# The right half of slice 0's G: from the software queue with a cast to SP's queue and a rounding on VectorE

## The chip, the cores and the metric

The kernel runs on one core of a Trainium2 chip. The metric is the device time of one execution in microseconds. Before the change the median of three runs is 163.8 us (163.7 to 163.8). The profile is one execution, recorded by the hardware profiler.

## The reference

The gradient of a weight, summed over batch and rows:

```
input       : (16, 512, 1024) float32      X, seen as 8192 x 1024
grad_output : (16, 512, 768)  float32      G, seen as 8192 x 768
grad_weight = einsum('bmk,bmn->kn', input, grad_output)      1024 x 768, float32
```

So it is one matrix product, X transposed times G, contracted over 8192 rows. The kernel multiplies in bf16 and accumulates in float32.

## The kernel before, in words

**Slices and units.** The 8192 rows are cut into 64 slices of 128 rows; two neighbouring slices make a unit (32 units). A slice of X is 128 x 1024 (512 KB in float32), a slice of G 128 x 768 (384 KB). The output is split into quarters: A and B are the left half of X's columns with the left and the right half of G's, C and D the right half of X's with the left and the right half of G's. Each quarter has four blocks of 128 x 384, one per PSUM bank, and two quarters are open at a time.

**Two kinds of units.** `LOADS` (line 12) gives the first seven and the last two units the kind "s": each slice is multiplied as it is. The other 23 are of kind "P": VectorE forms sums and differences of the unit's quarters (lines 126 to 155), and seven products, named A, D, m, n, o, p and q, take the place of eight.

**The order.** `ORDER` (line 16) is a list of visits written out by hand. "C2:4!0,0,0,0" opens quarter C, brings it up to item 2 (slices 0 and 1), lets ScalarE empty 4 of its banks, and closes it. The first visits are A1 (slice 0), D1 (slice 0, left open), C2 (slices 0 and 1), B2 (slices 0 and 1), D3 (slices 1 and 2), A2, B4, A3, C4 and A4; D5 is the first to use slice 4 (unit 2) and B7 the first to use slice 6 (unit 3). A visit to one slice is four matmuls, to two slices eight. In C2 the first matmul uses slice 0, the second slice 1, and so on in turn. Work on TensorE, VectorE, ScalarE and GpSimd (POOL) goes in the order in which it is written (line 77). When a quarter is closed, each bank is emptied by a copy or an addition (lines 295 to 304).

**The loads.** From unit 2 on, POOL issues one transfer of G and one of X for each unit, float32 in memory and bf16 in SBUF (lines 105 and 106): this is queue q0, the software queue, in the profile. Slices 1 to 3 of G and slices 2 and 3 of X come the same way, slice by slice (lines 112 and 114). The start is different. X of slices 0 and 1 and the left half of slice 0's G come in float32 over hardware queues, into the staging tiles `xf` and `gf` (lines 79 to 83): the left half of G and then X of slice 1 from SP (queue q1), X of slice 0 from ScalarE (queue q10). They are rounded to bf16 by VectorE and ScalarE (`round_by`, line 205; for slice 0 in lines 210 to 216, for slice 1 in lines 362 to 365 just before C2). The right half of slice 0's G is the first transfer of POOL (line 110) and is rounded on the way in.

**The start of TensorE.** Twelve matmuls on constants (`WARMUP`, line 88) run while the first loads are under way. Then A1 needs the left half of slice 0's X and of its G, D1 the right halves of both, C2 the right half of X and the left half of G of slices 0 and 1, and B2 the other halves of the same two slices.

Of the kernel before, what the change touches and what calls it, by code (L numbers as in the profile page):

```python
# [9 lines left out]
P = 128  # L10
# [32 lines left out]
def kernel(  # L43
# [6 lines left out]
    nc = tc.nc  # L50
# [4 lines left out]
    _, _, N = grad_output.shape  # L55
    S = B * M // P
    KH = K // 2
    NH = N // 2
# [3 lines left out]
    G = grad_output.rearrange("b m n -> (b m) n")  # L62
# [17 lines left out]
    gf = pairs.tile([P, N], f32, name="gf", tag="gp")  # L80
    nc.sync.dma_start(out=gf[:, 0:NH], in_=G[0:P, 0:NH])
    nc.scalar.dma_start(out=xf[0], in_=X[0:P, :])
    nc.sync.dma_start(out=xf[1], in_=X[P : 2 * P, :])

    ones = nc.const_aps.tensor(1.0, (P, P), bf16)
# [13 lines left out]
    for u, kind in enumerate(LOADS):  # L99
        pool = pairs if u else head  # L100
        xp = pool.tile([P, 2, K], bf16, name="xp", tag="xp")
        gp = pool.tile([P, 2, N], bf16, name="gp", tag="gp")
        if u >= MERGED:
            rows = slice(2 * u * P, 2 * (u + 1) * P)
            nc.gpsimd.dma_start(out=gp, in_=G[rows, :].rearrange("(p m) n -> p m n", m=2))  # L105
            nc.gpsimd.dma_start(out=xp, in_=X[rows, :].rearrange("(p m) k -> p m k", m=2))  # L106
        for h in range(2):
            s = 2 * u + h
            if s == 0:
                nc.gpsimd.dma_start(out=gp[:, 0, NH:N], in_=G[0:P, NH:N])  # L110
            if s > 0 and u < MERGED:
                nc.gpsimd.dma_start(out=gp[:, h, :], in_=G[s * P : (s + 1) * P, :])
            if s > 1 and u < MERGED:
                nc.gpsimd.dma_start(out=xp[:, h, :], in_=X[s * P : (s + 1) * P, :])
            if kind == "s":
                items.append(("s", xp[:, h, :], gp[:, h, :]))
        if kind == "P":
            items.append(("P", xp, gp))
        xg.append((xp, gp))
# [79 lines left out]
    def fill(n):  # L199
        for _ in range(n):  # L200
            f, i = filler.pop()
            f(i)


    def round_by(engine, dst, src, c0, c1):
        copy = nc.vector.tensor_copy if engine == "DVE" else nc.scalar.copy
        copy(out=dst[:, c0:c1], in_=src[:, c0:c1])

    x0, x1, g0 = items[0][1], items[1][1], items[0][2]
# [144 lines left out]
    for n, step in enumerate(ORDER):  # L354
        step, _, ahead = step.partition("!")
        step, _, byact = step.partition(":")
        byact, first = byact[:1], byact[1:]
        at = next(c for c in step if c.isalpha())
        before, upto = step.split(at)
        if not rounded and done[at] < 2 <= int(upto):  # L360
            rounded = True
            round_by("DVE", x1, xf[1], 4 * P, 6 * P)
            round_by("ACT", x1, xf[1], 6 * P, 8 * P)
            round_by("DVE", x1, xf[1], 0, 2 * P)
            round_by("ACT", x1, xf[1], 2 * P, 4 * P)
        fill(int(before or 0))
        ahead = [int(a) for a in ahead.split(",")] if ahead else None
        visit(at, int(upto), int(byact or 0), first, ahead is not None, ahead, n == len(ORDER) - 1)
# [31 lines left out]
```

## Time and profile before

| what | us |
|---|---|
| median of three runs | 163.8 |
| the profiled execution's own time | 163.8 |
| span of the profiled execution, first to last instruction | 162.0 |
| PE busy | 156.6 |
| VectorE (DVE) busy | 139.1 |
| ScalarE (ACT) busy | 94.5 |
| POOL busy | 35.2 |
| DMA, mean rate of what was written | 206 GB/s |

The granted TensorE clock is 1.000 over the whole span. Times in the views are microseconds from the start of the span. A row of the timeline has the start, the duration, the engine, the line, the operation, what it writes and reads, the shape and the count; in brackets stands the idle time before it and what ended it. PE is the row of matmuls and PEld that of weight loads; matmuls overlap, so each is longer than the distance from one to the next. A row of the table by stretches has, for each stretch, its length and the busy time (and number) of PE, PEld, DVE, ACT and POOL, and then the granted clock, the mean busy share of the 16 DMA engines and the GB/s that they wrote. As the software queue writes bf16 for float32 that it reads, its reading rate is twice what it writes. A row of a DMA queue has packets, MB written, and the share of the stretch.

### The profile page before, as it was taken

The numbers are of one execution on the slowest core, as the hardware profiler recorded it, in microseconds if no ns is written. First come the engines' busy times: TensorE is split into PE (matmuls) and PEld (weight loads), VectorE is DVE, ScalarE is ACT, GpSimd is POOL, SyncE is SP. The second block draws the span as 40 slices with busy tenths as digits, with TensorE's granted clock in tenths as the row PEclk, the third lists the DMA queues.
The fourth block names the chain that finished last, engine by engine and source line by source line (L and its number), as shares of the span: only waits on it lengthen the run. The fifth ranks groups of instructions, "written<-read, shape, count | busy, mean of one in ns | idle before, by whom it ended". The sixth has DMA issues, their size and how long they took to land.

```text
span 162.0 us, 2752 instructions
## 1 busy us (share of the span) xinstructions
PE 156.6 (97%) x951; PEld 92.5 (57%) x951; DVE 139.1 (86%) x288; ACT 94.5 (58%) x221; POOL 35.2 (22%) x70
## 2 busy tenths in 40 slices
PE   8699999999999999999999999999999999999992
PEld 3365556566655565655656666666555666666661
DVE  0457837478979999999989999999998999999992
ACT  3776004745587799359749684561447646888410
POOL 7552222212222211222221222222212100000000
PEclk9999999999999999999999999999999999999999
DMA  5999999999999999999999999999999999902674
GB/s 173 270 210 213 213 215 214 211 211 216 215 212 210 213 211 212 214 212 214 214 214 212 212 218 214 214 208 212 211 211 217 212 212 214 182 4 97 230 283 167
DMA packets 12397, 33.30 MB, mean 206 GB/s; under 512 B 1376, under 2 KB 4192, under 8 KB 12384
## 3 DMA queue, kind: packets, MB, share of 16 engines
q0 software_dynamic: 9504, 28.74, 89.8%
q1 hardware_dynamic: 2592, 3.80, 6.6%
q10 hardware_dynamic: 288, 0.59, 1.0%
q8 instruction: 7, 0.11, 0.3%
q14 instruction: 6, 0.05, 0.1%
HBM read 58.72 MB, written 3.15 MB: 382 GB/s over the span
## 4 chain that ended last, share of the span: by engine, by line
PE 93%; DMA 4%; issue 0%; DVE 0%; POOL 0%; POOLq 0%
PE bank L286 92%; DMA gp<-in_grad_output_dram 4%; PE bank L337 0%; DVE acc L345 0%; POOL gp L110 0%; POOLq L384 0%
## 5 line engine op out<-in xcount | busy, mean ns | idle before, releaser
L286 PEld LDWEIGHTS <-xp 128*128 128x128 bf16 x649 | 63.2, 98 | 44.4 <-issue 1.6
L286 PE MATMUL bank<-gp,xp 128*128 128x384 bf16 x468 | 81.0, 326 | 1.4 <-DMA gp<-in_grad_output_dram 0.8
L300 ACT COPY macc<-bank 128x384 f32<-128x384 f32 x73 | 31.5, 493 | 25.0 <-PE bank L286 24.9
L304 DVE TENSOR_TENSOR acc<-bank,acc 128x384 f32<-128x384 f32 x69 | 34.7, 552 | 9.0 <-PE bank L286 8.6
L286 PEld LDWEIGHTS <-xe 128*128 128x128 bf16 x276 | 26.6, 98 | 18.5 <-DVE xe L146 0.8
L286 PE MATMUL bank<-ge,xp 128*128 128x384 bf16 x181 | 33.6, 326 | 0.0
L286 PE MATMUL bank<-gp,xe 128*128 128x384 bf16 x184 | 32.4, 326 | 0.0
L267 ACT COPY bank<-macc 128x384 f32<-128x384 f32 x56 | 25.4, 503 | 8.0 <-DVE macc L304 6.9
L300 ACT COPY acc<-bank 128x384 f32<-128x384 f32 x44 | 19.5, 486 | 15.4 <-PE bank L286 15.1
L106 POOL DMA_DIRECT2D xp<-in_input_dram x30 | 15.9, 530 | 51.2 <-DMA xp<-in_input_dram 29.0
L105 POOL DMA_DIRECT2D gp<-in_grad_output_dram x30 | 15.9, 530 | 38.9 <-DMA gp<-in_grad_output_dram 17.4
L304 DVE TENSOR_TENSOR macc<-bank,macc 128x384 f32<-128x384 f32 x44 | 22.5, 552 | 1.4 <-PE bank L286 1.2
L267 ACT COPY bank<-acc 128x384 f32<-128x384 f32 x34 | 15.2, 492 | 8.8 <-DVE acc L304 8.7
L286 PE MATMUL bank<-ge,xe 128*128 128x384 bf16 x92 | 16.7, 326 | 0.0
L146 DVE TENSOR_TENSOR xe<-xp 128x1024 bf16<-128x1024 bf16 x23 | 15.7, 683 | 0.2 <-DMA xp<-in_input_dram 0.2
L155 DVE TENSOR_TENSOR xp<-xp 128x1024 bf16<-128x1024 bf16 x23 | 15.7, 683 | 0.0
L190 DVE TENSOR_TENSOR acc<-acc,macc 128x768 f32<-128x768 f32 (+1 forms) x20 | 14.6, 791 | 0.0
L132 DVE TENSOR_TENSOR ge<-gp 128x768 bf16<-128x768 bf16 x23 | 12.7, 551 | 0.1
L141 DVE TENSOR_TENSOR gp<-gp 128x768 bf16<-128x768 bf16 x23 | 12.7, 550 | 0.0
L150 DVE TENSOR_TENSOR xe<-xp 128x512 bf16<-128x512 bf16 x23 | 9.6, 418 | 0.0
L136 DVE TENSOR_TENSOR ge<-gp 128x384 bf16<-128x384 bf16 x23 | 8.1, 351 | 0.0
L302 DVE COPY acc<-bank 128x384 f32<-128x384 f32 x6 | 3.1, 553 | 3.2 <-PE bank L286 3.1
(21 smaller groups left out, 22.2 us busy)
## 6 DMA issues: line engine op xcount, KB each, us to landing
xp<-in_input_dram POOLq DMA_DIRECT2D x30, 512.0 KB, 16.8
gp<-in_grad_output_dram POOLq DMA_DIRECT2D x30, 384.0 KB, 16.7
out_dram<-acc SPq DMA_DIRECT2D x15, 192.0 KB, 1.9
gp<-in_grad_output_dram POOLq DMA_DIRECT2D x3, 192.0 KB, 6.3
xf<-in_input_dram ACTq DMA_DIRECT2D x1, 512.0 KB, 4.1
xf<-in_input_dram SPq DMA_DIRECT2D x1, 512.0 KB, 5.0
xp<-in_input_dram POOLq DMA_DIRECT2D x2, 256.0 KB, 7.6
gf<-in_grad_output_dram SPq DMA_DIRECT2D x1, 192.0 KB, 3.8
```

Of the source, the lines that this page charges most:

```text
L105: nc.gpsimd.dma_start(out=gp, in_=G[rows, :].rearrange("(p m) n -> p m n", m=2))
L106: nc.gpsimd.dma_start(out=xp, in_=X[rows, :].rearrange("(p m) k -> p m k", m=2))
L132: nc.vector.tensor_add(out=ge[:, 0:2, :], in0=g[:, :, 0, :], in1=g[:, :, 1, :])
L141: nc.vector.tensor_sub(out=g[:, 1:3, :], in0=g[:, 1:3, :], in1=g[:, 3::-3, :])
L146: nc.vector.tensor_add(out=xe[:, 0:2, :].rearrange("p a k -> p (a k)"), in0=xp[:, 0, :], in1=xp[:, 1, :])
L150: nc.vector.tensor_add(out=extra[i][0][:, 2, :], in0=xp[:, 0, 0:KH], in1=xp[:, 1, KH:K])
L155: nc.vector.tensor_sub(out=x[:, 1:3, :], in0=x[:, 1:3, :], in1=x[:, 0::3, :])
L190: op(out=dst, in0=dst, in1=src)
L267: nc.scalar.copy(out=bank, in_=sum_of(p, q))
L286: nc.tensor.matmul(bank, stat, mov, start=opening and j == 0 and not carried, stop=close and j == len(items_now) - 1, skip_group_check=car ...
L300: nc.scalar.copy(out=dst, in_=bank)
L304: nc.vector.tensor_add(out=dst, in0=bank, in1=dst)
```

## The change

The right half of slice 0's G no longer comes as POOL's first transfer with a cast. SP issues it, in float32, into the right half of the staging tile `gf`, behind the left half and ahead of X of slice 1. VectorE rounds it to bf16 as one instruction of 128 x 384, written just before the visit D1 (the second of `ORDER`, n = 1), so behind the copy of A1's first bank and ahead of the casts of X of slice 1. All else is as before.

```diff
     nc.sync.dma_start(out=gf[:, 0:NH], in_=G[0:P, 0:NH])
     nc.scalar.dma_start(out=xf[0], in_=X[0:P, :])
+    nc.sync.dma_start(out=gf[:, NH:N], in_=G[0:P, NH:N])
     nc.sync.dma_start(out=xf[1], in_=X[P : 2 * P, :])
...
             s = 2 * u + h
-            if s == 0:
-                nc.gpsimd.dma_start(out=gp[:, 0, NH:N], in_=G[0:P, NH:N])
             if s > 0 and u < MERGED:
                 nc.gpsimd.dma_start(out=gp[:, h, :], in_=G[s * P : (s + 1) * P, :])
...
         before, upto = step.split(at)
+        if n == 1:
+            round_by("DVE", g0, gf, NH, N)
         if not rounded and done[at] < 2 <= int(upto):
             rounded = True
             round_by("DVE", x1, xf[1], 4 * P, 6 * P)
```

## The prediction

> **What bounds the kernel now.** I read the page's shares first (PE 97% of the span, granted clock 1.0 throughout, so no clock question), then the chain of waits in order of time, because the whole edit lies in the first 8 us:
>
> ```profile
> 1.23 0.66 POOL gp L110
> 1.89 5.89 DMA gp<-in_grad_output_dram
> 7.78 0.04 issue
> 7.82 8.67 PE bank L286 x52
> 16.49 0.01 issue
> 16.51 141.17 PE bank L286 x864
> ```
>
> Up to 7.82 us the end hangs on POOL's loads of G; from there on on matmuls alone. Two things follow: a microsecond lost or won at 7.82 is carried to the end only if nothing later re-times PE, and the break in the chain at 16.49 is suspicious, because the chain does not say who was waited for there. PE's own timeline shows the start, one visit of slice 0 at a time:
>
> ```profile
> 5.18 0.82 PE L286 MATMUL bank<-gp,xp 128*128 128x384 bf16 x4 [0.55 <-DVE xp L207]
> 6.58 0.97 PE L286 MATMUL bank<-gp,xp 128*128 128x384 bf16 x5 [0.58 <-DMA gp<-in_grad_output_dram]
> 7.82 16.50 PE L286 MATMUL bank<-gp,xp 128*128 128x384 bf16 x99 [0.27 <-DMA gp<-in_grad_output_dram]
> ```
>
> A1 (four matmuls) runs at 5.18; D1 waits until 6.58 for the right half of slice 0's G, the transfer that the edit moves; D1's four and the first of C2 run; the sixth matmul waits until 7.82 for G of slice 1. Matmuls start every 0.1625 us (0.97 less one length of 0.326, over four steps, is 0.161), so that sixth one could have started at 6.58 + 5 x 0.1625 = 7.39: 0.43 us are lost there. The weight loads say what happens at 16.5:
>
> ```profile
> 16.50 4.18 PEld L286 LDWEIGHTS <-xp 128*128 128x128 bf16 x27 [0.40 <-DMA xp<-in_input_dram]
> 20.85 5.19 PEld L286 LDWEIGHTS <-xp 128*128 128x128 bf16 x33 [0.17 <-DMA xp<-in_input_dram]
> ```
>
> These are the first uses of X of unit 2 (D5, slice 4) and of unit 3 (B7, slice 6). Narrow windows around them, PE's row again:
>
> ```profile
> 15.68 1.49 PE L286 MATMUL bank<-gp,xp 128*128 128x384 bf16 x7
> 20.25 1.30 PE L286 MATMUL bank<-gp,xp 128*128 128x384 bf16 x7
> ```
>
> Seven matmuls need 6 x 0.1625 + 0.326 = 1.30. So at 16.5 PE lost 0.19 us to X of unit 2, and at 20.85 it lost nothing, but only just: the load that waited ended at 20.95, beside a matmul due at about 20.90. **PE is re-timed by the DMA stream twice after the start.** Last, whether that stream has room. Busy time and DMA by stretch, last two columns the DMA share and GB/s written:
>
> ```profile
> 2.50:4.00 1.50, 1.50 (x6) 0.58 (x5) 0.00 (x0) 0.00 (x0) 1.50 (x4) 1.00 0.99 374
> 4.00:5.25 1.25, 0.70 (x6) 0.28 (x4) 0.63 (x4) 0.69 (x3) 1.25 (x4) 1.00 1.04 419
> 5.25:6.00 0.75, 0.75 (x4) 0.37 (x5) 0.64 (x2) 0.62 (x3) 0.35 (x1) 1.00 1.15 205
> 6.00:7.80 1.80, 0.98 (x6) 0.48 (x5) 0.61 (x3) 1.56 (x5) 0.54 (x1) 1.00 1.14 202
> 7.80:16.50 8.70, 8.67 (x52) 4.98 (x51) 5.64 (x12) 5.69 (x13) 3.17 (x6) 1.00 1.11 213
> ```
>
> It has none: the share is 0.99 or more from 2.5 us on. From 5.25 on nearly all of it is the software queue, which writes bf16, so 202 to 213 written are 404 to 426 GB/s read. The queues of the first 5.25 us:
>
> ```profile
> q1 hardware_dynamic: 263, 0.68, 38.9%
> q10 hardware_dynamic: 144, 0.52, 26.0%
> ```
>
> There is no software packet yet, though POOL issued from 1.23.
>
> **The change, part by part.** The profiled execution took 163.8 us, 162.0 of span and 1.8 around it; the median of the runs is the same 163.8, so sums go against 163.8.
>
> *The right half of G comes over SP's queue.* 128 x 384 x 4 B = 0.197 MB. On the software queue it took 0.197/(404 to 426) = 0.46 to 0.49 us of the stream. On SP's it goes at the rate of 2.5 to 4.0, where half the packets were such short rows, 374 GB/s: 0.53; at the 419 of 4.0 to 5.25, 0.47. I take 0.53, nearest in shape. Net on the stream: -0.02 to +0.07, I take +0.05. It lands behind the left half (issued 0.74, 3.8 us to landing, so 4.54) at about 5.1, half a microsecond later.
>
> *X of slice 1 moves back one place on SP.* SP issues it 0.4 us later (the row of the first issue is 0.38), which does not count, as its packets began only when the left half was done. Before, it landed 5.0 us after 1.18, at 6.18. Now +0.47 to +0.53 if the software queue keeps yielding as it did up to 5.25: 6.7. If the software queue instead starts at 5.25 and takes half: X starts at 4.5, 0.31 MB are through by 5.25, the other 0.21 MB go at some 205 GB/s and need 1.0 us, so data end at 6.3, against about 5.6 before; landing 6.9. I take 6.8, bounds 6.6 to 7.1. C2's sixth matmul needs it rounded: DVE's 128x256 cast (0.29), so 7.15, at the latest 7.45. That is before the 7.82 of today.
>
> The Trainium skill, "DMA: Bandwidth & Descriptors", section "Queues, rings and completion order", says a DMA engine alternates packet by packet between the queues that have work; up to 5.25 us the rows above show no software packet. By the rule X of slice 1 lands nearer 6.9, by the row nearer 6.7; the sum is the same.
>
> *POOL loses its first issue.* L110 is 0.66 of POOL's time, so G of slice 1 is issued at 1.23 instead of 1.89, and everything behind it one place earlier. That buys no bytes: G of slice 1 landed at 7.78 when left G, X0, X1, right G and itself had all passed. The same five have to pass now, in another order, through a full stream. So G of slice 1 lands at 7.78 + 0.05, or up to 0.25 earlier if it shares with X1 (its 0.39 MB no longer stand behind the right half, and some of X1 ends after it). POOL's later issues wait for the load eight places before; that distance stays.
>
> *DVE rounds the right half before D1.* 128x384 casts do not occur; 128x192 took 0.26, 128x256 0.29, 128x128 0.23, so by that slope 0.36 (bounds 0.33 and 0.52, twice the 192 one). It stands on DVE behind the copy of A1's first bank (5.55 + 0.56 = 6.11), which waits for PE, so it cannot start earlier though its data land at 5.1. DVE's next work began 0.1 after that copy, so the cast ends between 6.44 and 6.73, most likely 6.52; 0.05 more to PE (first cast of X0 to first weight load): D1 at 6.57, against 6.58. The wait for a DMA has become a wait for DVE, worth nothing. Behind it on DVE are the two casts of X of slice 1 (6.21 to 6.70 today): they slide to about 6.85 to 7.4, wanted at 7.4 and, for B2, after 9. DVE is then idle until 9.48 (the copy of two banks), so the 0.36 us vanish in that hole. ACT's casts of X1 (6.83 to 7.56) may slide 0.3 by the landing; the next ACT work, C2's banks, starts at 8.18.
>
> The Trainium skill, "SBUF — State Buffer", section "SBUF: two separate sides", speaks against this move: an fp32 SBUF copy on VectorE can keep GpSimd from writing its DMA descriptors. By that, up to 0.36 us of the software stream, and of the time, would be lost. In this trace two such casts lie at 6.21 to 6.70 inside a stretch whose DMA share is 1.14, so nothing starved.
>
> *Sum.* D1 0.0; C2's sixth matmul at 7.6 to 7.85, -0.2 to 0.0; unit 2's X at 16.50 + 0.05, where the start's gain is waited away; unit 3's X at 20.85 + 0.05, again just in time; after that PE runs as before. End +0.05: 163.85, written 163.8. Own range 163.6 to 164.1.
>
> **Rivals.**
> *Slower, X of slice 1 becomes last.* If X1 lands after G1, PE waits for its cast. It costs only above 7.82 + 0.19 (what 16.5 absorbs), that is a landing after 8.01 - 0.29 - 0.06 = 7.66. Against it: my upper bound is 7.1. If X1 were served last of the five, with landing at 7.83 plus the 0.4 by which landings trail data, C2 resumes at 8.58: +0.76 - 0.19 = +0.57, 164.4. Chance 0.10.
> *Slower, the stream itself.* The added short rows break the stream (the first packets, 2.0 to 2.5, ran at share 0.80 and 199 GB/s). At 199 the right half costs 0.99 us, +0.5 on units 2 and 3: 164.3. Against it: that row is the ramp. Chance 0.10.
> *Faster, the move fills holes.* SP's queue starts its packets early, and the slices 2.0 to 2.5 (share 0.80) and the hand-over at 5.25 hold perhaps 0.15 us idle. If all 0.46 of the right half left the stream, unit 2 and 3 came 0.4 earlier and the 0.43 at 7.82 with them: 163.4. Against it: those holes are smaller than that. Chance 0.10.
> *No re-timing.* G1 comes 0.2 earlier and units 2 and 3 too, by 0.2: 163.6, inside my case.
>
> **Numbers.** My case, with "no re-timing", has 0.70. A measurement here tells about 0.2% (0.33 us) from no change. My case is within it but for some 0.03 above; both slower rivals are above, the faster one is below: faster 0.11, same 0.67, slower 0.22. The range runs from 163.5 to 164.2, which leaves out the far ends of the rivals, some 2 in 10.
>
> **What the profile would show.** D1 waiting for DVE's cast, near 6.57; X of slice 1 landing at 6.6 to 7.1; the sixth matmul still waiting for G of slice 1, at 7.6 to 7.85; the weight load at 16.5 still waiting for X, longer than 0.40 if the start gained; the one at 20.85 within 0.1 of its place. Wrong if the 7.8 wait names DVE's cast of X instead, or if the waits at 16.5 and 20.85 vanish (the stream won time) or grow by over 0.3 (it lost).

## The result: 0.6 us slower, and the profile after

The changed kernel takes 164.38 us (median of four runs, 164.29 to 164.44), the kernel before 163.75 beside it (163.58 to 163.80): ratio 1.0040, 95% interval 1.0022 to 1.0057. The forecast was 163.8, in a range of 163.5 to 164.2; the kernel is slower, outside it. The profiled execution took 164.29 (span 162.5) against 163.8 (162.0). In the longer series of the experiments some executions, of the kernel before among them (five of 25 in one series, 165.1 to 165.5), take some 1.5 us longer, which widens the intervals.

The chain of waits of the changed kernel, in order of time, says at once what took the place of the loads of G:

```profile
1.65 6.50 DMA xf<-in_input_dram
8.15 0.02 issue
8.18 0.31 DVE xp L206
8.48 0.05 issue
8.53 149.68 PE bank L285 x916
```

It is X of slice 1: issued by SP at 1.65, landed at 8.15, then VectorE's cast, then matmuls to the end. Before, it landed at 1.18 + 5.0 = 6.2 and stood nowhere in the chain. PE's timeline of the changed kernel, and below it VectorE's:

```profile
5.17 0.82 PE L285 MATMUL bank<-gp,xp 128*128 128x384 bf16 x4
6.42 0.97 PE L285 MATMUL bank<-gp,xp 128*128 128x384 bf16 x5 [0.43 <-DVE gp L206]
8.53 15.67 PE L285 MATMUL bank<-gp,xp 128*128 128x384 bf16 x95 [1.13 <-DVE xp L206]
```

```profile
5.55 0.56 DVE L301 COPY acc<-bank 128x384 f32<-128x384 f32 x1 [0.17 <-PE bank L285]
6.02 0.35 DVE L206 CAST gp<-gf 128x384 bf16<-128x384 f32 x1
8.18 0.50 DVE L206 CAST xp<-xf 128x256 bf16<-128x256 f32 x2 [1.80 <-DMA xf<-in_input_dram]
```

A1 is where it was. D1 starts at 6.42 instead of 6.58: the moved cast did no harm. But C2's first matmul on slice 1 starts at 8.53 instead of 7.82, and VectorE sat idle for 1.80 us ahead of its casts. The weight loads behind it no longer stop for X of unit 2 or unit 3, where they had waited 0.40 and 0.17 us:

```profile
8.53 15.45 PEld L285 LDWEIGHTS <-xp 128*128 128x128 bf16 x96 [1.52 <-DVE xp L206]
```

So PE is 0.71 us late at 8.53, takes back the 0.18 that it used to lose to X of unit 2 (the matmul there started 0.176 us late), and is 0.53 late from there to the end. That is the difference of the two profiled executions, 0.5.

Why the transfer is late is read in the DMA queues. Two answers for the first 4.9 us, the kernel before and then the changed one; columns are packets, MB written, and share of the stretch:

```profile
q1 hardware_dynamic: 225, 0.53, 33.7%
q10 hardware_dynamic: 144, 0.52, 27.9%
```

```profile
q10 hardware_dynamic: 144, 0.52, 27.8%
q1 hardware_dynamic: 288, 0.39, 27.0%
q0 software_dynamic: 41, 0.06, 7.8%
```

Before, SP's queue (q1) has moved 0.53 MB by then: the left half of G (0.20) and 0.33 of X of slice 1. The software queue (q0) has moved nothing. In the changed kernel SP's queue has moved the two halves of G, 0.39 MB, and nothing of X; the software queue is already at work. The stretch from 4.9 to 7.5 us, before and then changed:

```profile
q0 software_dynamic: 370, 0.42, 94.9%
q1 hardware_dynamic: 63, 0.19, 19.4%
```

```profile
q0 software_dynamic: 187, 0.26, 55.7%
q1 hardware_dynamic: 138, 0.52, 52.0%
```

Before, only the rest of X of slice 1 (0.19 MB) was left for this stretch; in the changed kernel the whole of it runs here, alongside the software queue, at about half the engines' time. The packets of the trace say when each began: the software queue at 5.26 before and at 4.48 after; X of slice 1 ran from 4.01 to 5.76 before and from 4.94 to 7.71 after. Its 0.52 MB took 1.7 us then and 2.8 now. What the loads had read together by 7.5 us is the same, 2.09 MB in both.

### The profile page after: what moved, and what is told of

It is laid out like the page before. It is cut to its first block, busy times and chain, and to the rows that moved or that the text cites. A ratio compares the mean times of both kernels' runs of the same rounds, so it can differ in the third digit from the quotient of the medians.

```text
span 162.5 us, 2755 instructions
## 1 busy us (share of the span) xinstructions
PE 157.0 (97%) x951; PEld 92.5 (57%) x951; DVE 139.3 (86%) x289; ACT 94.5 (58%) x221; POOL 34.6 (21%) x69
## 4 chain that ended last, share of the span: by engine, by line
PE 93%; DMA 4%; DVE 1%; SPq 0%; issue 0%
PE bank L285 92%; DMA xf<-in_input_dram 4%; PE bank L336 0%; DVE acc L344 0%; SPq L83 0%; SPq L81 0%; DVE xp L206 0%
## 5 line engine op out<-in xcount | busy, mean ns | idle before, releaser
L89 PE MATMUL bank<-const-bfloat16-1.0 128*128 128x512 bf16 (+1 forms) x12 | 4.5, 559 | 0.8 <-PEq L385 0.8
```

## The experiments

**Theory of turns.** In the changed kernel the software queue's first packet comes at 4.48 us (4.38 in a second profile of it), so it is taken to be ready soon after 4.3. If X of slice 1 has begun on SP's queue by then, it passes first and the software queue starts behind it. If the right half of G is still there, the software queue gets its turn before X, which then shares from its first packet on. **Rivals:** the hardware queue is slow behind the short rows of G; the new cast on VectorE is what costs; the removal of POOL's first load lets the software queue in.

All times in the table are in us. "X1" is the landing of X of slice 1, "sixth" the start of C2's first matmul on slice 1, "lost" what PE then lost to X of unit 2. "Worked out" is 163.8 + (sixth - 7.82) + (lost - 0.18), to be held against the profiled execution beside it.

| kernel | X1 | sixth | lost | worked out | profiled | median of all runs | ratio, 95% interval |
|---|---|---|---|---|---|---|---|
| before | 6.19 | 7.82 | 0.18 | 163.8 | 163.80 | 163.75 | |
| changed | 8.15 | 8.53 | 0 | 164.33 | 164.29 | 164.38 | 1.0022 to 1.0057 |
| changed, again | 8.11 | 8.48 | 0 | 164.28 | 164.23 | 164.39 | 0.9987 to 1.0053 |
| POOL late, three memsets | 6.66 | 7.78 | 0.19 | 163.77 | 163.69 | 164.04 | 1.0002 to 1.0070 |
| POOL late, two memsets | 7.96 | 8.69 | 0.22 | 164.71 | 164.63 | 164.61 | 1.0021 to 1.0071 |
| right half also ahead of X1, before | 8.06 | 8.43 | 0.10 | 164.33 | 164.29 | 164.39 | 0.9999 to 1.0065 |
| X1 ahead of right half | 6.25 | 8.96 | 0 | 164.76 | 164.70 | 166.87 | 1.0135 to 1.0270 |
| right half on ScalarE's queue | 6.80 | 8.34 | 0 | 164.14 | 164.08 | 164.12 | 1.0002 to 1.0063 |
| X1 on ScalarE's queue | 7.04 | 7.48 | 0.20 | 163.48 | 163.44 | 163.65 | 0.9957 to 1.0022 |
| X1 on ScalarE's queue, POOL late | 6.63 | 7.62 | 0.21 | 163.63 | 163.61 | 163.68 | 0.9969 to 1.0027 |
| extra cast, before | 6.08 | 7.58 | 0.17 | 163.55 | 163.56 | 163.66 | 0.9970 to 1.0010 |

The sum holds within 0.1 us for every kernel of the table (experiments 7 and 9 are told below): the time is set by when slice 1 can be used, with unit 2's X as a floor. Medians are to be compared with the 163.70 to 163.75 of the kernel before. Two kernels have a median of 164.39 and an interval that reaches 1: the ten times of "changed, again" lie at 164.22 to 164.62, those of the third experiment are spread over 163.93 to 165.87.

**1. POOL starts later.** In the changed kernel, three memsets ahead of POOL's loads.

```diff
+    idle = accp.tile([P, 384], f32, name="idle")
+    for _ in range(3):
+        nc.gpsimd.memset(idle, 0.0)
     items = []
```

> The changed kernel with three memsets of 128x384 on POOL ahead of its first load, so that the software queue starts later; from VectorE's 128x384 copies (0.35 to 0.56 us) an estimate of 1.0 to 1.6 us later. Theory of turns: in the changed kernel the software queue sent its first packet at 4.48 us, before X of slice 1 had begun (4.94), and shared the DMA engines with it from then on. If it starts after 4.94, X of slice 1 passes first, lands near 6.7 instead of 8.15, the sixth matmul starts at 7.7 to 8.0 when G of slice 1 is there, and the time is 163.7 to 163.9. Rival, the hardware queue itself is slow behind the short rows of the right half: X of slice 1 still lands near 8, time 164.3 or more.

The chain of waits of this kernel is that of the kernel before again, with G of slice 1 in it and not X:

```profile
2.04 5.70 DMA gp<-in_grad_output_dram
7.74 0.04 issue
7.78 8.67 PE bank L289 x52
16.45 0.02 issue
16.48 141.17 PE bank L289 x864
```

POOL's first load is issued at 2.04 instead of 1.23, 0.8 us later where 1.0 to 1.6 was expected; the software queue's first packet is at 5.72, X of slice 1 runs from 4.35 to 6.33 and lands at 6.66, with the short rows still ahead of it on SP's queue. This rules out a queue that is slow behind short rows: nothing on SP's queue was changed. The profiled execution is back at 163.69. The timed ones are not quite: median 164.04, six of ten at 163.9 to 164.2 and three at 165.4 to 165.5. Why they stay behind the profile is open.

**2. Two memsets instead of three.**

> As the kernel with three memsets on POOL, with two: POOL's first load is issued near 1.6 us instead of 1.23 (changed) or 2.04 (three memsets). Theory of turns: on each DMA engine it decides whether X of slice 1 has begun when the software queue gets ready, near 4.9 here, against 4.35 to 4.9 for the end of the right half; on most engines it has, so X of slice 1 lands at 6.6 to 7.2, the sixth matmul starts at 7.6 to 7.9, 163.7 to 164.1. Rival, the landing of X of slice 1 follows the start of the software queue in proportion (8.1 at 1.23, 6.7 at 2.04): 7.4 to 7.6, and the sixth matmul at 7.8 to 8.0, 163.8 to 164.1.

Neither the times of the theory nor those of the rival came. POOL's first load was issued at 1.57, the software queue's first packet came at 4.95, and X of slice 1 landed at 7.96. G of slice 1 landed later still, 8.65, and it ended PE's wait:

```profile
8.69 15.57 PE L289 MATMUL bank<-gp,xp 128*128 128x384 bf16 x93 [1.06 <-DMA gp<-in_grad_output_dram]
```

Of the 128 packets of X, 125 had begun by 6.54, the last only at 7.32; X of unit 2 landed 0.9 us later than before (17.38), though the loads together had read only 0.08 MB less by 16 us (5.60 MB, against 5.68). Every load ends in 16 packets of 4 bytes, and X of slice 1 lands 0.3 to 0.4 us after the last of them in all these profiles. Here 14 of its 16 came by 6.67, in time for the landing that the theory forecast (6.6 to 7.2), and the last two at 7.17 and 7.64. That some of the 16 DMA engines fell behind here fits the numbers, but the trace doesn't name the engine of a packet, so how the landing changes between an issue at 1.23 and one at 2.04 stays open.

**3. The right half ahead of X in the kernel before.** POOL's first load and its cast stay and are used; the float32 copy on SP is read by nobody.

```diff
     nc.scalar.dma_start(out=xf[0], in_=X[0:P, :])
+    nc.sync.dma_start(out=gf[:, NH:N], in_=G[0:P, NH:N])
     nc.sync.dma_start(out=xf[1], in_=X[P : 2 * P, :])
```

> The kernel before, POOL's first load with its cast kept and used, plus the float32 right half of G on SP ahead of X of slice 1, which nobody reads. Theory of turns: X of slice 1 has not begun when the software queue gets ready, so that queue starts at about 4.5 instead of 5.26 and X of slice 1 lands at 8.0 to 8.5; 0.5 us more of transfers also make X of units 2 and 3 later by 0.4 to 0.6; sixth matmul 8.4 to 8.9, time 164.3 to 164.8. Rival, it is the removal of POOL's first load that lets the software queue in early: X of slice 1 lands near 6.7, the software queue starts at 5.2 to 5.8, and only the 0.5 us of transfers show, 163.9 to 164.2.

Its chain of waits is that of the changed kernel:

```profile
1.64 6.42 DMA xf<-in_input_dram
8.06 0.02 issue
8.08 0.31 DVE xp L208
8.39 0.04 issue
8.43 149.80 PE bank L287 x916
```

X of slice 1 lands at 8.06 and the software queue starts at 4.58. POOL issues what it did before, VectorE has no new cast; the place of X on SP's queue alone brings the whole loss of the profile (164.29, as in the changed kernel; the timed runs, with an interval from 0.9999, only just say so). X of unit 2 was 0.55 later (17.01 against 16.46), within what was expected, and cost PE only 0.10, since PE was late itself.

**4. One more cast in the kernel before.**

```diff
+        if n == 1:
+            spare = accp.tile([P, NH], bf16, name="spare")
+            nc.vector.tensor_copy(out=spare, in_=gf[:, 0:NH])
```

> The kernel before with one more cast of 128x384 on VectorE, from the staged left half of G into a spare tile, where the changed kernel has its new cast. Theory: it vanishes in VectorE's idle time, 163.7 to 163.8. Rival, the cast itself is what costs (0.35 us, through the casts of X of slice 1 that stand behind it, or by holding up POOL): 164.1.

```profile
6.03 0.35 DVE L362 CAST spare<-gf 128x384 bf16<-128x384 f32 x1
```

163.66: no loss. The cast is innocent where it stands; POOL was not issuing then (its row in this profile is empty from 5.6 to 6.7 us). This execution also shows how far the same loads wander from run to run: its sixth matmul started at 7.58, 0.24 earlier than in the profile of the kernel before.

**5. X of slice 1 ahead of the right half, on SP.**

```diff
-    nc.sync.dma_start(out=gf[:, NH:N], in_=G[0:P, NH:N])
     nc.sync.dma_start(out=xf[1], in_=X[P : 2 * P, :])
+    nc.sync.dma_start(out=gf[:, NH:N], in_=G[0:P, NH:N])
```

> The changed kernel with X of slice 1 issued on SP ahead of the right half of G. Theory of turns: X of slice 1 begins at 4.0 as in the kernel before and lands near 6.2; the right half now shares with the software queue and lands at 6.7 to 7.2, its cast ends at 7.1 to 7.6, D1 starts there, and C2's first use of slice 1 follows 0.81 us later, at 8.0 to 8.4: time 163.9 to 164.2. Rival, the cast on VectorE or the loss of POOL's first issue makes the kernel slow and not the place of X: 164.4 as in the changed kernel, with X of slice 1 landing late again.

X of slice 1 lands at 6.25 and the software queue starts at 5.32, as in the kernel before. Now the right half comes late, at 7.71, and D1 waits for its cast:

```profile
5.21 1.32 PE L285 MATMUL bank<-gp,xp 128*128 128x384 bf16 x4
8.15 16.15 PE L285 MATMUL bank<-gp,xp 128*128 128x384 bf16 x98 [1.62 <-DVE gp L206]
```

Whoever stands second behind X shares with the software queue and pays: these 0.2 MB land 2.5 us later than in the changed kernel (5.25), where X's 0.5 MB landed 2.0 later than before. The landing was expected at 7.2 at most, and the time at 163.9 to 164.2. The four timed values are 164.70 (profiled), 166.65, 167.09 and 168.07, far above what the profile explains; experiment 9 returns to that.

**6. The right half behind X of slice 0 on ScalarE's queue.**

```diff
-    nc.sync.dma_start(out=gf[:, NH:N], in_=G[0:P, NH:N])
+    nc.scalar.dma_start(out=gf[:, NH:N], in_=G[0:P, NH:N])
```

> The changed kernel with the right half of G issued on ScalarE's queue behind X of slice 0, so that X of slice 1 is second on SP's queue again. Theory of turns: X of slice 1 begins at 4.0, has begun when the software queue gets ready, and lands at 6.2 to 6.8; the right half lands at 5.5 to 6.3; D1 starts at 6.5 to 6.8, the sixth matmul at 7.5 to 7.9 (G of slice 1): 163.6 to 163.9. Rival, any 0.2 MB more on the hardware queues make X of slice 1 late: landing near 8, 164.3.

X of slice 1 began at 3.88 and landed at 6.80, at the end of what was expected, but the right half landed at 7.09 instead of 6.3 at most, so D1 started at 7.53:

```profile
7.53 16.80 PE L285 MATMUL bank<-gp,xp 128*128 128x384 bf16 x102 [1.52 <-DVE gp L206]
```

164.12: a miss on the time, and a limit of the theory. The right half's first packet came at 4.34, ahead of the software queue's (5.27), and it was late all the same: only 51 of its 128 rows had begun by 5.27, beside 90 of the 128 of X. Two transfers on the two hardware queues share as well, and what is left of them then shares with the software queue.

**7. X of slice 1 in two halves of its columns, the needed one first.**

```diff
-    nc.sync.dma_start(out=xf[1], in_=X[P : 2 * P, :])
+    nc.sync.dma_start(out=xf[1][:, KH:K], in_=X[P : 2 * P, KH:K])
+    nc.sync.dma_start(out=xf[1][:, 0:KH], in_=X[P : 2 * P, 0:KH])
```

> The changed kernel with X of slice 1 issued as two transfers of half the columns on SP, the right half (which C2 needs) first. Theory of turns: sharing from the start, 0.26 MB pass in half the time of 0.52: the right half lands at 6.4 to 7.0, the left one near 8.1, where B2 needs it only after 9; the sixth matmul starts at 7.6 to 7.9, 163.6 to 163.9. Rival, what counts is that X of slice 1 stands behind the short rows at all: right half at 7.5 or later, 164.1 or more.

The right half landed at 8.05, hardly earlier than the whole had (8.15), and the left one at 9.91. VectorE's casts wait for both:

```profile
8.07 0.29 DVE L207 CAST xp<-xf 128x256 bf16<-128x256 f32 x1 [1.48 <-DMA xf<-in_input_dram]
9.93 0.30 DVE L207 CAST xp<-xf 128x256 bf16<-128x256 f32 x1 [1.56 <-DMA xf<-in_input_dram]
```

165.32 (profiled 165.47, ratio 1.0039 to 1.0175). The forecast by bytes, 6.4 to 7.0, failed for the landing, but not for most of the transfer: of the 16 packets of 4 bytes that end the right half, 11 came at 6.25 to 6.55, the others up to 7.70, where those of the whole X in the changed kernel came at 7.05 to 7.82. So most of the half was earlier, and the landing waited for its last part. Whole X and each half have the same 128 rows (4 KB and 2 KB), so a sharing by packets would fit the late part; no run here tests that by itself. The second loss came from ScalarE: its cast of the left half stands ahead of its copies of C2's banks, and PE waited 1.0 us more, until 10.76, for a bank.

**8. X of slice 1 behind X of slice 0 on ScalarE's queue**, alone and with POOL late by three memsets.

```diff
-    nc.sync.dma_start(out=xf[1], in_=X[P : 2 * P, :])
+    nc.scalar.dma_start(out=xf[1], in_=X[P : 2 * P, :])
```

> The changed kernel with X of slice 1 issued on ScalarE's queue behind X of slice 0, while the right half of G stays second on SP's queue. Theory of turns: X of slice 1 begins at 4.4 when X of slice 0 is through, before the software queue gets its turn, and lands at 6.3 to 7.0; the right half lands near 5.3; D1 near 6.45, the sixth matmul at 7.5 to 7.9: 163.6 to 163.9. Rival, all bytes on the hardware queues count alike: X of slice 1 near 8 and 164.3.

> X of slice 1 on ScalarE's queue behind X of slice 0, and three memsets on POOL ahead of its first load. If a start of the software queue behind X of slice 1 is all that is wanted, X of slice 1 lands at 6.3 to 6.7 and the sixth matmul starts at 7.5 to 7.8, but the load of X of unit 2 lands at 16.2 to 16.5 as before and the gain is waited away: 163.6 to 163.9. If the start does carry through, below 163.4.

Without the memsets X of slice 1 began at 4.24, behind X of slice 0, and landed at 7.04, the right half at 5.95; both are later than expected (7.0 at most, near 5.3), as they share with each other, and D1 starts at 6.65. The sixth matmul starts at 7.48, right behind the fifth, 0.34 us earlier than before. The chain of waits and the weight loads show where that goes:

```profile
6.65 9.50 PE bank L285 x57
16.15 0.04 issue
16.19 141.18 PE bank L285 x864
```

```profile
16.19 4.18 PEld L285 LDWEIGHTS <-xp 128*128 128x128 bf16 x27 [0.42 <-DMA xp<-in_input_dram]
20.52 3.42 PEld L285 LDWEIGHTS <-xp 128*128 128x128 bf16 x22 [0.16 <-DMA xp<-in_input_dram]
```

PE waits again for X of unit 2, and X of unit 3 is again just in time. That is the floor that the prediction named. The whole stream happened to be 0.3 us earlier in this execution (unit 2 at 16.15, against 16.46 and, in experiment 4, 16.22), which is run-to-run wander, so the profiled 163.44 is no gain: the medians are 163.65 and 163.68 against 163.71. The right half of G can come over SP's queue at no loss if X of slice 1 is not behind it; nothing tried here beats the kernel before.

**9. TensorE kept busy.** Experiment 5 with six matmuls on constants, unused, between A1 and D1.

```diff
+            for _ in range(6):
+                nc.tensor.matmul(
+                    wps,
+                    ones,
+                    nc.const_aps.tensor(1.0, (P, 512), bf16),
+                    start=True,
+                    stop=True,
+                )
```

> The kernel with X of slice 1 ahead of the right half, with six matmuls of 512 columns on constants between A1 and D1, where TensorE idled 1.7 us in its profile. That kernel's profiled execution took 164.70 us and its timed ones 166.65 to 168.07, and in its profile the matmuls of A1 stood 0.32 us apart instead of 0.16. Theory: TensorE falls back to, or stays at, that half pace when it idles so long at the start, by different amounts in different executions; filled, the timed executions fall to 163.9 to 164.9. Rival, the spread has another cause (DMA): the median stays above 166.

The median fell from 166.87 (four values, 164.70 to 168.07) to 165.09 (ten values, 164.80 to 165.58; ratio 1.0047 to 1.0106), a little above what was expected, because the right half landed at 7.93 here and D1 started at 8.38. The spread went from 3.4 to 0.8 us. The kernel before took 163.70 beside the first and 163.72 beside the second, so the fall does not come from their being timed apart: the idle time of TensorE had a price of its own, apart from the delay. That it is the half pace was not seen: no execution of 166 us or more was profiled, and in the profile of the filled kernel TensorE had reached full pace by 3.7 us, ahead of the six matmuls (5.83).

## Why the prediction was wrong

- **What bounds the kernel.** Right: PE from 7.82 on, re-timed by X of unit 2. The 0.18 us lost there came back as a cushion, and the sums in the table confirm it. At unit 3 no matmul was late in any of these profiles. "Granted clock 1.0 throughout" was not so for the first microseconds (last section); A1's matmuls stand 0.17 us apart in both profiles, so nothing of the difference comes from it.
- **The cast on VectorE at no cost.** Right, shown by experiment 4. It took 0.35 (0.36 forecast) and D1 started at 6.42 (6.57 forecast), as the cast began at 6.02, a little ahead of the end of the copy's row (6.11), not behind it. The rule of the Trainium skill ("SBUF — State Buffer", section "SBUF: two separate sides") that such a cast can hold up POOL's descriptors showed nothing here, but POOL was not issuing at that time either (in the changed kernel not from 5.60 to 7.85), so this is no test of it.
- **The stream conserves its bytes.** Right: 2.09 MB read by 7.5 us in both. X of units 2 and 3 landed 0.15 later (16.61 and 20.96), forecast 0.05.
- **G of slice 1 up to 0.25 earlier.** 7.57 instead of 7.78 in the profile of the changed kernel, but 7.93 in the second one of it, so that it came earlier at all was luck.
- **X of slice 1 lands at 6.8, bounds 6.6 to 7.1.** This is the step that failed; it landed at 8.15, and C2's sixth matmul, in the sum at -0.2 to 0.0, came 0.71 us later. I took the start of the software queue at 5.25 as a fixed time, or as yielding until the hardware queues were empty. It was neither: that start had itself been made by X of slice 1, which had begun at 4.01. With another transfer in its place the software queue began at 4.48. Then 0.52 MB at half of 410 GB/s need 2.6 us from 4.94, so 7.5, and 0.4 more to the landing: the same arithmetic with the right start would have said 7.9 to 8.0.
- **The rival "X of slice 1 becomes last" was what happened**, nearly to the number: C2 resumed at 8.53 (8.58 forecast), +0.53 on the profile (0.57), 164.38 (164.4). Its number came from the bytes alone, with X through last of the first five loads. That the software queue would start ahead of X and share from X's first packet on was not in it, so the reason is not the rival's. I gave it 0.10, "against it: my upper bound is 7.1", an upper bound that rested on the one assumption. The three chances after it are also off by 0.01: by their own parts they would be 0.10, 0.67 and 0.23.
- **The Trainium skill, "DMA: Bandwidth & Descriptors", section "Queues, rings and completion order".** It says that an engine drains a packet of several descriptors from one queue and then turns to the next queue that has work. I weighed it only from 5.25 on and wrote that the sum is the same. The runs agree with it in kind: the software queue gets in at 4.48, ahead of X, when SP's queue is between transfers, and behind X (5.26, 5.32) when X has begun.

## What to carry to other kernels

The time at which a queue starts to move data may be made by what another queue is doing, so a start read from a trace is no constant once the edit touches that other queue; ask what would have gone out in that moment instead. On a full DMA stream the bytes are conserved and the order is not: list what each wait needs, and ask of each transfer that is moved back whether it still begins before the bulk queue does, and what it shares the engines with from there. A gain or loss at the start is to be followed to the next place where PE waits for a load, as that is where it is cut off.

## What the runs showed of the hardware that I had not expected

- A transfer that had begun before the software queue, and had the engines nearly to itself, passed almost undisturbed (0.52 MB in 1.7 us); one that began after it took 2.8 us. Beside another hardware queue the head start was worth less (experiments 6 and 8: begun at 4.34 and 4.24, landed at 7.09 and 7.04).
- A landing can be made by a small part of a load. In experiment 7 half of X landed at 8.05 though 11 of its 16 closing packets had come by 6.55; in experiment 2 everything from G of slice 1 to X of unit 2 landed 0.9 us late, though the total read was only 0.08 MB behind. One or two straggling engines would fit, but the trace doesn't name them.
- TensorE works at half pace at the start of an execution, and the end of that differs between executions. The 512-column warm-up matmuls start 0.427 us apart at first; in the kernel before this changes to 0.22 at 3.7 us, in the changed one the matmuls are at full pace from about 5.0, in experiment 5 A1's four still stand 0.32 apart up to 6.17 (they took 1.32 us, above, against 0.82). The views show a granted clock of 1.00 all the while, but the trace's own record of that clock begins, at full clock, only at 3.65, 5.00 and 6.23 us in these three profiles; what lies ahead of it the views count as full. Over all 13 profiles it begins at 3.62 to 6.23. The Trainium skill, "TensorE: Matmul & The Clock Gate", "Part 1: The HAM clock gate", describes such a start at half rate with a free-running window; that TensorE falls back to it when it idles would fit experiment 9, but no profile here caught it.
